# First projection in written order on all five streams, with two raw token tiles, GpSimd scaling the others, and norm weights as columns

## The chip, the core and the metric

The kernel runs on one core of one Trainium2 chip. A core has five instruction streams that run beside each other and wait for each other through semaphores: PE (matmuls, with its weight loads PEld), DVE, ACT, POOL (GpSimd) and SP, which here mostly issues DMAs. The metric is the device time of one execution in microseconds (us); the time of the kernel before is the median of 3 runs.

## The reference

One layer of a decoder block over 1024 tokens of width 1024. Cut to what matters for the change:

```python
h = rmsnorm(x, norm_mix[layer])          # x * rsqrt(mean(x*x) + 1e-6) * g
[q, k/v per NSA branch, gates, rq, rk, rv, rg, gate_a, gate_b] = split(h @ w_in[layer])
q  = rotary(q, positions, 16, 500000.)   # also the NSA keys
rq, rk = rotary(rq, positions, 128, 10000.), rotary(rk, ...) * 128**-0.5
ret = retention(rq, rk, rv)              # chunks of 128 tokens, per-head normalised
ret_out = silu(rg) * ret
mix = sigmoid(gate_a) * (nsa_out @ w_proj_a) + sigmoid(gate_b) * (ret_out @ w_proj_b)
x = x + mix @ w_out
x = x + square(relu(rmsnorm(x, norm_mlp) @ w_up)) @ w_down
y = rmsnorm(x, norm_final)
```

The change concerns the beginning: the first RMSNorm, and `h @ w_in` for the retention heads 0 and 1 (their q and k: "first projection"; their v and g: "second projection").

## The kernel before

**Tiles.** The 1024 tokens are eight tiles of 128 (`NT`), the width 1024 is eight blocks of 128 (`KD`). The normalised input is kept transposed for the whole kernel in two buffers, `bh` and `bl`: `bh` is the value rounded to the matmul's format, `bl` the remainder. Every weight is split the same way into `wh` and `wl` (`chunk_weights`, 512 KB at a time, two width blocks each). A product of float32 accuracy is then three matmuls per width block: bh·wh, bh·wl, bl·wh, so that one token tile against 512 columns is 24 matmuls of 128x512 (`dense_tok`).

**Normalisation of a tile.** `load_norm` loads 128 rows of x. `norm_tile` squares them on ACT with a sum per row (L199), has GpSimd turn the sum into 1/rms (`rstd_of`, `msq` L193 and `rstd` L194), and has DVE multiply x by it and by the gain in one instruction (L203, `h`, 128x1024). The gain is a row, broadcast to all 128 partitions by a DMA of 512 KB (`load_gain`). `to_big` transposes h on PE in eight blocks (L209), four to a PSUM bank `tp`; ACT writes `bh` (L212) and DVE `bl` (L213).

**First projection.** Loop over the eight token tiles. Tiles 0 and 1 advance together, two width blocks at a time, as the weights arrive; `to_big` of tile j+1 stands on PE ahead of the matmuls of tile j. The 128x512 result is scaled by ACT into `xq` (L305, four heads, with the factors `small`), and rotated on DVE into `qk` (`rot_ret`, L314 to L317: two products of 128x512, two sums of 128x256). The rotation's cosines and sines come from tables that GpSimd makes from the positions in `table_steps`: `ang`, `num`, three pairs of `prd` and `ang`, then a clip on DVE, two sines on ACT, and two more GpSimd operations. The retention's tables have 128x512 elements; those of the NSA heads (`cosn`, `sinn`, needed long after) have 128x64.

**Second projection.** Per tile: four width blocks of matmuls, the score matmuls of the tile before (`pS`, `ret_s`), the transposition of `qk` (`ret_t`, split by ACT and DVE into `qkT`, L322/L323), the retention output (`ret_o`), and the other four width blocks. Its weights `w_r0b` are loaded and split by `chunk_weights` after the last tile of the first projection.

**What sets the order.** At the start, 17 warm-up matmuls on zeros run ahead of the data. Inside `manual_schedule` (the first three weight steps of tiles 0 to 2) PE and POOL keep the order in which the code is written; DVE, ACT and SP are ordered by a scheduler there. Behind it the scheduler orders all five. Every engine executes its stream in order, so an instruction that waits holds back all behind it.

Of the kernel before, what the change touches and what calls it, by code (L numbers as in the profile page):

```python
# [111 lines left out]
def hybrid_block(ctx: ExitStack, tc: tile.TileContext, a: dict, out: bass.AP):  # L112
# [84 lines left out]
    def norm_a(x, o, pool):  # L197
        ssq = pool.tile([P, 1], F32, name="ssq", tag="ssq")
        A.activation(o, x, AF.Square, accum_out=ssq)  # L199
        return rstd_of(ssq, D, pool)  # L200

    def norm_b(x, r, gain, o):
        V.scalar_tensor_tensor(o, x, r, gain, op0=OP.mult, op1=OP.mult)  # L203

    def to_big(h, j, ps):
        for q in range(2):
            tp = ps.tile([P, 4, P], F32, name="tp", tag="tp")
            for k in range(4):
                T.transpose(tp[:, k], h[:, (4 * q + k) * P:(4 * q + k + 1) * P], ident)  # L209
            js = slice(j * P, (j + 1) * P)  # L210
            ks = slice(4 * q, 4 * q + 4)
            A.activation(bh[:, ks, js], tp, AF.Copy)  # L212
            V.tensor_sub(bl[:, ks, js], tp, bh[:, ks, js])  # L213

    def load_gain(src, pool, name):
        g = pool.tile([P, D], F32, name=name, bufs=1)
        nc.sync.dma_start(g, src.to_broadcast([P, D]))
        return g

# [23 lines left out]
    with ExitStack() as es:  # L243
        psA = es.enter_context(tc.tile_pool(name="psA", bufs=2, space=PSUM, reuse_waits="tile"))
        tabs = es.enter_context(tc.tile_pool(name="tabs", bufs=1, reuse_waits="tile"))
        cret = tabs.tile([P, 6 * P], F32, name="cret")[:, :P + 512 + 72]
# [8 lines left out]
        with ExitStack() as e1:  # L255
# [21 lines left out]

            def table_steps(part):
                pos = nrm.tile([P, NT], F32, name="pos")
                V.tensor_copy(pos, pos_i)  # L280
                inv0 = P + 512
                for half, off, cos, sin in (((64, 0, cosr, sinr), (8, 64, cosn, sinn))[part],):
                    shp = [P, NT, half]
                    ang = tmp.tile(shp, F32, name=f"ang{half}", tag="t1")
                    num = tmp.tile(shp, F32, name=f"num{half}", tag="t2")
                    prd = tmp.tile(shp, F32, name=f"prd{half}", tag="t1")
                    G.tensor_tensor(ang, pos[:, :, None].to_broadcast(shp),
                                    cret[:, None, inv0 + off:inv0 + off + half].to_broadcast(shp), op=OP.mult)
                    G.tensor_scalar(num, ang, 1.0 / TWO_PI, MAGIC, op0=OP.mult, op1=OP.add)
                    for pc in (PC1, PC2, PC3):  # L290
                        if pc == PC2:
                            yield
                        G.tensor_scalar(prd, num, -MAGIC, -pc, op0=OP.add, op1=OP.mult)
                        G.tensor_tensor(ang, ang, prd, op=OP.add)
                    yield
                    V.tensor_scalar(ang, ang, PI_LO, -PI_LO, op0=OP.min, op1=OP.max)
                    A.activation(sin, ang, AF.Sin)
                    A.activation(num, ang, AF.Sin, scale=0.5)
                    G.tensor_mul(num, num, num)
                    G.tensor_scalar(cos, num, -2.0, 1.0, op0=OP.mult, op1=OP.add)  # L300

            def rot_ret(ps, j, s0, o):
                xq = tmp.tile([P, 512], F32, name="xq")
                for h in range(4):
                    A.activation(xq[:, h * P:(h + 1) * P], ps[:, h * P:(h + 1) * P], AF.Copy,  # L305
                                 scale=small[:, s0 + h:s0 + h + 1])
# [94 lines left out]
            warm = nrm.tile([P, 512], mybir.dt.bfloat16, name="warm", bufs=1)  # L401
            V.memset(warm, 0.0)
            wps = psA.tile([P, 512], F32, name="mm", tag="mm")
            for i in range(WARM):
                mm(wps, warm[:, :P], warm, True, True)
            with tc.manual_schedule(engines={mybir.EngineType.PE, mybir.EngineType.Pool}):
# [1120 lines left out]
```

## Time and profile before

| | |
|---|---|
| median of 3 runs | 1585.05 us (1584.82 to 1585.37) |
| profiled execution | 1585.19 us |
| its span | 1583.4 us |
| granted TensorE clock, mean | 0.995 |
| PE busy | 98% of the span |
| DVE / ACT / POOL busy | 68% / 46% / 27% |

The page's second part shows the same thing by fortieths of the span: PE stands at 7 tenths in the first fortieth and at 9 or more in all others, and PEclk, the granted TensorE clock, at 8 tenths in the first and at 9 or more after it. A fortieth is 39.6 us. Times below count from the start of the span. In the list of groups, a row is: line, engine, operation, output<-inputs, shape, count | busy us, mean ns of one | idle before it and what released it.

### The profile page before, as it was taken

Reading aid. Unit: us, or ns where it says so; the run is one execution under the profiler, and the core shown is the slowest. Engines: PE = TensorE matmul, PEld = TensorE weight load, DVE = VectorE, ACT = ScalarE, POOL = GpSimd, SP = SyncE. Lnnn points to the kernel's source line nnn. Section 1 sums busy time; section 2 is a strip of 40 time slices with the busy share of each in tenths; the row PEclk is TensorE's granted clock in tenths of the full one; section 3 lists DMA queues with packets and bytes.
Section 4 is the critical chain, followed back from the end, with each engine's and each line's share of the span. In section 5 each row is a group of like instructions: output and inputs, shape, how many; then the busy total and the mean of one; then the engine's idle time right before and its main releaser. Section 6 shows DMA issues by size and latency. Waiting matters only on the chain.

```text
span 1583.4 us, 22723 instructions
## 1 busy us (share of the span) xinstructions
PE 1551.3 (98%) x7847; PEld 1297.6 (82%) x7847; DVE 1078.8 (68%) x2208; ACT 730.4 (46%) x1643; POOL 421.2 (27%) x502
## 2 busy tenths in 40 slices
PE   7999999999999999999999999999999999999998
PEld 5888887887888888888888888788888888888886
DVE  5765565683777777776665378777777667876673
ACT  5454454573676776666622144222222244443452
POOL 4111010000332333233100000655554436521320
PEclk8999999999999999999999999999999999999999
DMA  6102101252111111211453332444444497664472
GB/s 224 52 29 67 53 18 43 67 180 70 54 38 45 54 47 34 61 48 61 154 179 118 133 130 89 157 154 159 153 154 159 169 375 252 212 221 121 144 268 98
DMA packets 99363, 191.83 MB, mean 121 GB/s; under 512 B 26864, under 2 KB 30320, under 8 KB 99248
## 3 DMA queue, kind: packets, MB, share of 16 engines
q1 hardware_dynamic: 98144, 187.50, 35.8%
q0 software_dynamic: 560, 1.84, 0.3%
q8 instruction: 62, 1.02, 0.3%
q10 hardware_dynamic: 544, 1.05, 0.2%
q14 instruction: 53, 0.43, 0.1%
HBM read 140.02 MB, written 50.33 MB: 120 GB/s over the span
## 4 chain that ended last, share of the span: by engine, by line
PE 86%; DVE 5%; issue 3%; ACT 3%; POOL 2%; DMA 1%; SPq 0%; POOLq 0%; ACTq 0%; DVEq 0%
PE mmu L159 22%; PE mm L159 20%; PE mmd L159 19%; PE gps L159 9%; PE S L159 4%; PE O L159 3%; PE pt L893 2%; PE pt L892 2%; ACT pW L848 1%; PE pO L159 1%; DVE S L839 1%; PE pc L159 1%; DVE pl L895 1%; ACT pS L848 0%; PE pD L159 0%
## 5 line engine op out<-in xcount | busy, mean ns | idle before, releaser
L1046 DVE TENSOR_TENSOR wl<-raw,wh 128x1024 fp32r<-128x1024 f32 x121 | 182.3, 1531 | 66.6 <-ACT wh L1045 65.1
L1045 ACT ACTIVATE wh<-raw 128x1024 fp32r<-128x1024 f32 x121 | 125.2, 1056 | 206.5 <-PE mmd L159 121.8
L159 PE MATMUL mm<-wh,bh 128*128 128x512 f32 (+1 forms) x448 | 175.6, 392 | 1.2 <-ACT n L580 1.0
L159 PE MATMUL mm<-wh,bl 128*128 128x512 f32 (+1 forms) x448 | 170.2, 380 | 4.8 <-DVE bl L213 4.7
L159 PE MATMUL mmd<-wh 128*128 128x512 f32 x448 | 174.3, 389 | 0.0
L159 PE MATMUL mmd<-wl,wh 128*128 128x512 f32 x448 | 174.3, 389 | 0.0
L159 PE MATMUL mmd<-wh,wl 128*128 128x512 f32 x448 | 174.3, 389 | 0.0
L159 PE MATMUL mm<-wl,bh 128*128 128x512 f32 (+1 forms) x448 | 169.7, 379 | 0.0
L895 DVE TENSOR_TENSOR pl<-pt,ph 128x512 fp32r<-128x512 f32 (+1 forms) x160 | 103.7, 648 | 32.1 <-ACT ph L894 30.1
L894 ACT ACTIVATE ph<-pt 128x512 fp32r<-128x512 f32 (+1 forms) x160 | 90.3, 567 | 55.8 <-PE pt L893 53.9
L839 DVE CUSTOM_DVE_ANT_0 S<-S,edge_m 128x512 f32<-128x512 f32 (+3 forms) x192 | 100.6, 529 | 14.2 <-PE S L159 12.5
L857 POOL TENSOR_SCALAR pS<-pS,cf 128x1024 f32<-128x1024 f32 (+7 forms) x64 | 47.9, 748 | 229.5 <-DVE cf L855 78.2
L159 PE MATMUL gps<-bh,wh 128*128 128x512 f32 x256 | 108.2, 423 | 0.3 <-ACT gst L750 0.2
L159 PEld LDWEIGHTS mm<-wh,bl 128*128 128x128 f32 x448 | 84.8, 189 | 22.2 <-DVE bl L213 5.8
L1127 POOL TENSOR_TENSOR sf<-raw 128x512 f32<-128x512 f32 x14 | 22.7, 1623 | 297.2 <-DVE wl L1046 291.9
L159 PE MATMUL gps<-bl,wh 128*128 128x512 f32 x256 | 100.5, 393 | 0.0
L159 PE MATMUL gps<-bh,wl 128*128 128x512 f32 x256 | 100.5, 392 | 0.0
L159 PE MATMUL mmu<-bh,wh 128*128 128x512 f32 x256 | 99.7, 389 | 0.0
L159 PE MATMUL mmu<-bl,wh 128*128 128x512 f32 x256 | 99.6, 389 | 0.0
L159 PE MATMUL mmu<-bh,wl 128*128 128x512 f32 x256 | 99.6, 389 | 0.0
L159 PEld LDWEIGHTS mmd<-wl,wh 128*128 128x128 f32 x448 | 84.1, 188 | 17.6
L159 PEld LDWEIGHTS mmd<-wh,wl 128*128 128x128 f32 x448 | 84.1, 188 | 17.5
(322 smaller groups left out, 4005.8 us busy)
## 6 DMA issues: line engine op xcount, KB each, us to landing
raw<-u_scr SPq DMA_DIRECT2D x56, 512.0 KB, 4.1
raw<-w_down SPq DMA_DIRECT2D x41, 512.0 KB, 4.7
raw<-w_up SPq DMA_DIRECT2D x32, 512.0 KB, 3.6
u_scr<-u SPq DMA_DIRECT2D x60, 256.0 KB, 2.2
u_scr<-s SPq DMA_DIRECT2D x45, 256.0 KB, 2.0
y<-w_down SPq DMA_DIRECT2D x14, 512.0 KB, 8.3
x<-x SPq DMA_DIRECT2D x8, 512.0 KB, 3.6
qt<-q_scr SPq DMA_DIRECT2D x32, 128.0 KB, 2.4
```

The costliest lines, as they stand in the source:

```text
L159: T.matmul(o, w, m, start=start, stop=stop)
L839: V.tensor_tensor_reduce(sc, sc, mk, -0.125, BIGPOS, OP.add, OP.min, mx[:, b:b + 1])
L848: A.activation(o, sc, AF.Exp, bias=mx[:, m:m + 1], scale=-1.0, accum_out=sums[:, b:b + 1])
L857: G.tensor_scalar(v, v, cf[:, b:b + 1], 1.0, op0=OP.mult, op1=OP.mult)
L892: T.transpose(tp[:, bi * 2], p0, ident)
L893: T.transpose(tp[:, bi * 2 + 1], p1, ident)
L894: A.activation(ph[:, :n], tp[:, :n], AF.Copy)
L895: V.tensor_sub(pl[:, :n], tp[:, :n], ph[:, :n])
L1045: A.activation(h[:, :n], r, AF.Copy)
L1046: V.tensor_sub(l[:, :n], r, h[:, :n])
L1127: eng.tensor_tensor(F[:, 1], x11, x21, op=OP.subtract)
```

## The change

- PE, GpSimd, DVE, ACT and SP all keep the written order to the end of the first projection; the scheduler takes over with the second.
- x is transposed before the gain is applied. The gain comes as 8 rows of 128, is transposed once on PE into eight columns (`gcols`), and DVE multiplies the transposed block by it (`put_half`, `y`, 128x512 twice per tile). ACT then rounds `y` into `bh`, DVE writes `bl` (`split_half`). The 512 KB broadcast is gone.
- Tiles 2 to 7 are multiplied by 1/rms in place by GpSimd (`scale_tile`, 128x1024) ahead of the transposition. DVE's `h` is gone.
- Tiles 0 and 1 are transposed unscaled. Their 1/rms enters where results leave PSUM: in `scaled_x` as a product of `small` with 1/rms (GpSimd), in `ret_v`, and in `rh`. In the second projection, `renorm` puts the factor into `bh` and `bl` of tiles 0 and 1 once their matmuls there are done: GpSimd adds the two parts, DVE multiplies by a transposed row of 1/rms, ACT and DVE split again.
- Warm-up matmuls are 8 and 5 instead of 17. Four x buffers instead of two. Three small loads go out from ACT's queue. Tiles 2, 3, 6 and 7 accumulate in PSUM banks of the retention stage.
- The loads and splits of `w_r0b` are placed by hand: the first at tile 4, the other three at the end, two of them ahead of the rotation of tile 6 and one ahead of that of tile 7.

```diff
-            def norm_tile(j, x):
-                h = nrm.tile([P, D], F32, name="h", bufs=HB)
-                norm_b(x, norm_a(x, h, nrm), gain1, h)
-                return lambda: to_big(h, j, psA)
...
+            def rstd(x):
+                ssq = nrm.tile([P, 16], F32, name="ssq", tag="ssq")[:, :1]
+                A.activation(warm, x, AF.Square, accum_out=ssq)
+                return rstd_of(ssq, D, nrm)
...
+            def put_half(x, j, q):
+                tp = psA.tile([P, 4, P], F32, name="tp", tag="tp")
+                for k in range(4):
+                    T.transpose(tp[:, k], x[:, (4 * q + k) * P:(4 * q + k + 1) * P], ident)
+                y = nrm.tile([P, 4, P], F32, name="y")
+                V.tensor_tensor(y, tp, gcols[:, 4 * q:4 * q + 4, None].to_broadcast([P, 4, P]), op=OP.mult)
+                return y
+
+            def split_half(y, j, q):
+                at = (slice(None), slice(4 * q, 4 * q + 4), slice(j * P, (j + 1) * P))
+                A.activation(bh[at], y, AF.Copy)
+                return lambda: V.tensor_sub(bl[at], y, bh[at])
+
+            def scale_tile(x):
+                G.tensor_scalar(x, x, rstd(x), 1.0, op0=OP.mult, op1=OP.mult)
+
+            def put_tile(j, x):
+                ys = [put_half(x, j, q) for q in range(2)]
+                for lo in [split_half(y, j, q) for q, y in enumerate(ys)]:
+                    lo()
+
+            def renorm(j):
+                js = slice(j * P, (j + 1) * P)
+                tp = psA.tile([P, 4, P], F32, name="tp", tag="tp")
+                T.transpose(tp[:, 0], rs_raw[j].to_broadcast([P, P]), ident)
+                rb = tp[:, :1].to_broadcast([P, 4, P])
+                for q in range(2):
+                    ks = slice(4 * q, 4 * q + 4)
+                    y = tmp.tile([P, 4, P], F32, name="yr", tag="xq")
+                    G.tensor_tensor(y, bh[:, ks, js].bitcast(F32), bl[:, ks, js].bitcast(F32), op=OP.add)
+                    V.tensor_tensor(y, y, rb, op=OP.mult)
+                    A.activation(bh[:, ks, js], y, AF.Copy)
+                    V.tensor_sub(bl[:, ks, js], y, bh[:, ks, js])
...
+            def scaled_x(ps, j, s0):
                 xq = tmp.tile([P, 512], F32, name="xq")
+                sc = small[:, s0:s0 + 4]
+                if s0 == 8 and j < RAW:
+                    sc = sm_raw[j]
+                    G.tensor_scalar(sc, small[:, s0:s0 + 4], rs_raw[j], 1.0, op0=OP.mult, op1=OP.mult)
                 for h in range(4):
...
+                for j in range(2, NT):
+                    if j < NT - 1:
+                        put_tile(j + 1, xs[j + 1])
+                    if j > 2:
+                        banks.append(bank(j))
+                    if j == 3:
+                        ws.append(w_dma(0, "w_r0b"))
+                        W2 = []
...
+                    if j == 4:
+                        w_hi(ws[0])
+                        W2 += w_lo(ws[0])
+                    dense_tok(banks[j], j, W)
+                    if j + 2 < NT:
+                        scale_tile(xs[j + 2])
+                    if j + 4 < NT:
+                        xs.append(load_norm(j + 4))
+                    if j == 3:
+                        for _ in table_steps(1):
+                            pass
...
+                    rotate(scaled_x(banks[j - 2], j - 2, 8), j - 2)
+                for i in (1, 2):
+                    w_hi(ws[i])
+                    W2 += w_lo(ws[i])
+                rotate(scaled_x(banks[6], 6, 8), 6)
+                w_hi(ws[3])
+                W2 += w_lo(ws[3])
+                rotate(scaled_x(banks[7], 7, 8), 7)
...
-                    v, y = ret_v(j, ps)
+                    v, y = ret_v(j, c, ps)
+                    if c == 0 and 0 < j <= RAW:
+                        renorm(j - 1)
```

What this does to the streams is shown at three places. A row is line, operation, output<-inputs, elements; the numbers in names tell buffers apart.

**GpSimd between the scaling of x for tile 4 and that for tile 6, after the change.** x_335 and x_337 are the inputs of tiles 4 and 5, ssq_540 belongs to tile 6; ang8, num8, prd8 are the NSA tables; the two rows that write fac_108 from small_94 are the factors for `xq` of tile 0 and of tile 1.

```order
L274 TENSOR_SCALAR x_335<-x_335,rstd_391 128x1024
L321 TENSOR_SCALAR fac_108<-small_94,fac_108 128x4
L192 TENSOR_SCALAR msq_459<-ssq_457 128x1
L193 TENSOR_TENSOR rstd_460<-msq_459,nhalf_97 128x1
L274 TENSOR_SCALAR x_337<-x_337,rstd_460 128x1024
L301 TENSOR_TENSOR ang8_466<-pos_135,cret_107 128x64
...
L313 TENSOR_SCALAR cosn_111<-num8_467 128x64
L321 TENSOR_SCALAR fac_108<-small_94,fac_108 128x4
L192 TENSOR_SCALAR msq_542<-ssq_540 128x1
```

The same place before, where ssq_489 and ssq_550 are the row sums of two neighbouring tiles:

```order
L193 TENSOR_SCALAR msq_491<-ssq_489 128x1
L194 TENSOR_TENSOR rstd_492<-msq_491,nhalf_97 128x1
L287 TENSOR_TENSOR ang8_374<-pos_372,cret_107 128x64
...
L300 TENSOR_SCALAR cosn_110<-num8_375 128x64
L193 TENSOR_SCALAR msq_552<-ssq_550 128x1
L194 TENSOR_TENSOR rstd_553<-msq_552,nhalf_97 128x1
```

The ten operations of the NSA tables stood between two tiles' 1/rms before; now the scaling and the factor for tile 1's `xq` stand around them, the factor behind all ten.

**ACT at the same place, after.** warm_128 is the scratch that the squares go to, mm_216 and pO_217 are the results of tiles 1 and 2, y_500 and y_507 the halves of tile 5, raw_429 the first part of `w_r0b`, x_395 the input of tile 6.

```order
L252 ACTIVATE warm_128,ssq_457<-x_337 128x1024
L310 ACTIVATE sinn_112<-ang8_466 128x64
L311 ACTIVATE num8_467<-ang8_466 128x64
L323 ACTIVATE xq_482<-mm_216,fac_108 128x128 x4
L343 ACTIVATE n_973<-qk_488 128x2x128
L270 ACTIVATE bh_92<-y_500 128x4x128
L270 ACTIVATE bh_92<-y_507 128x4x128
L455 ACTIVATE wh_431<-raw_429 128x1024
L252 ACTIVATE warm_128,ssq_540<-x_395 128x1024
```

Before, around the NSA sines (mm_390 and mm_451 are results of two neighbouring tiles, tp_435 and tp_442 the transposed halves of a tile):

```order
L305 ACTIVATE xq_416<-mm_390,small_94 128x128 x3
L297 ACTIVATE sinn_111<-ang8_374 128x64
L298 ACTIVATE num8_375<-ang8_374 128x64
L305 ACTIVATE xq_416<-mm_390,small_94 128x128
L212 ACTIVATE bh_92<-tp_435 128x4x128
L212 ACTIVATE bh_92<-tp_442 128x4x128
L199 ACTIVATE h_549,ssq_550<-x_510 128x1024
L305 ACTIVATE xq_477<-mm_451,small_94 128x128 x4
```

The square of the next tile stood behind `bh` before, too; now `xq` ahead of it takes a factor from GpSimd, `bh` comes from DVE's `y`, and a weight split and the rounding of a rotated `qk` (`n`) stand between.

**DVE where the second projection begins, after.** qkT_700 is the transposed `qk` of tile 0; the rows on t1_731 to qk_730, t1_747 to qk_746 and t1_761 to qk_760 rotate tiles 5, 6 and 7; wl_612, wl_671 and wl_724 are the second, third and fourth part of `w_r0b`.

```order
L344 TENSOR_TENSOR qkT_700<-tp_695,qkT_700 128x4x128
L335 TENSOR_TENSOR t1_731<-xq_725,cosr_109 128x512
...
L338 TENSOR_TENSOR qk_730<-t1_731,t2_732 128x4x64
L458 TENSOR_TENSOR wl_612<-raw_609,wh_611 128x1024
L458 TENSOR_TENSOR wl_671<-raw_668,wh_670 128x1024
L335 TENSOR_TENSOR t1_747<-xq_741,cosr_109 128x512
...
L338 TENSOR_TENSOR qk_746<-t1_747,t2_748 128x4x64
L458 TENSOR_TENSOR wl_724<-raw_721,wh_723 128x1024
L335 TENSOR_TENSOR t1_761<-xq_755,cosr_109 128x512
L336 TENSOR_TENSOR t2_762<-xq_755,sinr_110 128x512
```

Before, where t1_663 to qk_657 rotate tile 6, qkT_685 is that of tile 0, wl_714 to wl_726 are the first three parts of `w_r0b`, and t1_736 to qk_730 rotate tile 7:

```order
L314 TENSOR_TENSOR t1_663<-xq_658,cosr_108 128x512
...
L317 TENSOR_TENSOR qk_657<-t1_663,t2_664 128x4x64
L323 TENSOR_TENSOR qkT_685<-tp_680,qkT_685 128x4x128
L238 TENSOR_TENSOR wl_714<-raw_712,wh_713 128x1024
L238 TENSOR_TENSOR wl_720<-raw_718,wh_719 128x1024
L238 TENSOR_TENSOR wl_726<-raw_724,wh_725 128x1024
L314 TENSOR_TENSOR t1_736<-xq_731,cosr_108 128x512
```

Behind the first `qkT` stood three weight splits and one rotation; now three rotations and three splits stand there, alternating.

More of the change, by code (lines that the diff above doesn't have):

```diff
@@ L195, in rstd_of @@
         return r[:, :w]
[L197 to L218, printed above, removed]
     def dense_tok(o, j, W, k0=0, k1=KD, ticks=True):
@@ L278, in table_steps @@
-            def table_steps(part):
[L279 to L294, printed above, removed]
-                    yield
[L296 to L300, printed above, removed]
@@ new lines, in table_steps @@
+            def table_steps(part):
+                half, off, cos, sin = ((64, 0, cosr, sinr), (8, 64, cosn, sinn))[part]
+                inv0 = P + 512 + off
+                shp = [P, NT, half]
+                ang = tmp.tile(shp, F32, name=f"ang{half}", tag="t1")
+                num = tmp.tile(shp, F32, name=f"num{half}", tag="t2")
+                prd = tmp.tile(shp, F32, name=f"prd{half}", tag="t1")
+                G.tensor_tensor(ang, pos[:, :, None].to_broadcast(shp),
+                                cret[:, None, inv0:inv0 + half].to_broadcast(shp), op=OP.mult)
+                G.tensor_scalar(num, ang, 1.0 / TWO_PI, MAGIC, op0=OP.mult, op1=OP.add)
+                for pc in (PC1, PC2, PC3):
+                    yield
+                    G.tensor_scalar(prd, num, -MAGIC, -pc, op0=OP.add, op1=OP.mult)
+                    G.tensor_tensor(ang, ang, prd, op=OP.add)
+                yield
+                V.tensor_scalar(ang, ang, PI_LO, -PI_LO, op0=OP.min, op1=OP.max)
+                A.activation(sin, ang, AF.Sin)
+                A.activation(num, ang, AF.Sin, scale=0.5)
+                G.tensor_mul(num, num, num)
+                G.tensor_scalar(cos, num, -2.0, 1.0, op0=OP.mult, op1=OP.add)
+                yield
@@ L399, in ret_z @@
                 nc.sync.dma_start(b_scr[j, :, 2 * c:2 * c + 2], bt)
[L401 to L406, printed above, removed]
[L407 to L413 removed]
+            eng = mybir.EngineType
@@ L414, in hybrid_block @@
                 steps = table_steps(0)
                 next(steps)
-                W = chunk_weights("w_r0a", 512, 0, 1)
-                xt = load_norm(1)
-                put = norm_tile(1, xt)
-                next(steps, None)
-                first = [psA.tile([P, 512], F32, name="mm", tag="mm") for _ in range(2)]
-                dense_tok(first[0], 0, W, 0, 2)
-                put()
-                dense_tok(first[1], 1, W, 0, 2)
-                W += chunk_weights("w_r0a", 512, 1, 2)
@@ L425, in hybrid_block @@
-                xt = load_norm(2)
-                nc.sync.dma_start(small, a["c_small"])
-                for i in range(1, 4):
-                    if i > 1:
-                        W += chunk_weights("w_r0a", 512, i, i + 1)
-                    for j in range(2):
-                        dense_tok(first[j], j, W, 2 * i, 2 * i + 2)
-                    if i == 1:
-                        put = norm_tile(2, xt)
-                        xt = load_norm(3)
-                    if i == 2:
-                        put()
-                        next(steps, None)
@@ new lines, in hybrid_block @@
+                lb()
+                w_hi(ws[3])
+                next(steps)
+                W += w_lo(ws[3])
+                scale_tile(xs[3])
+                dense_tok(banks[0], 0, W, 4, 6)
+                y2 = [put_half(xs[2], 2, q) for q in range(2)]
+                dense_tok(banks[1], 1, W, 4, 6)
+                dense_tok(banks[0], 0, W, 6, 8)
+                l2 = [split_half(y, 2, q) for q, y in enumerate(y2)]
+                l2[0]()
+                l2[1]()
+                raw_factors(0, xs[0])
```

165 lines of the change are left out of this document (119 added, 46 removed).

## Prediction

> **What bounds the kernel now.** First the page, for the bound; then PE's list of waits over the first 160 us, since behind that point no stream of PE is altered.
>
> ```profile
> span 1583.4 us, 22723 instructions
> PE 1551.3 (98%) x7847; PEld 1297.6 (82%) x7847; DVE 1078.8 (68%) x2208; ACT 730.4 (46%) x1643; POOL 421.2 (27%) x502
> PE mm L159 <- DVE bl L213: 4.7, 1, 4.7
> PE tp L209 <- DVE h L203: 3.2, 2, 2.4
> ```
>
> PE is the bound: 32 us of the span are without it. Of what the change touches it waits 7.9 us (4.7 + 3.2), and pays for it once more in clock. The table by windows (start:end, length, busy of PE, PEld, DVE, ACT, POOL, granted clock, DMA) and PE's timeline (start, duration) show that:
>
> ```profile
> 8.59 1.09 PE L209 MATMUL tp<-ident,h 128*128 128x128 f32 x8 [0.84 <-DVE h L203]
> ...
> 11.54 0.40 PE L159 MATMUL mm<-wh,bl 128*128 128x512 f32 x1
> 14.33 1.94 PE L209 MATMUL tp<-ident,h 128*128 128x128 f32 x8 [2.40 <-DVE h L203]
> ...
> 22.03 0.80 PE L159 MATMUL mm<-wh,bl 128*128 128x512 f32 x1 [4.70 <-DVE bl L213]
> 13.00:14.00 1.00, 0.00 (x0) 0.00 (x0) 1.00 (x1) 0.66 (x1) 1.00 (x1) 0.77 0.36 147
> 14.00:27.00 13.00, 7.96 (x22) 5.99 (x23) 7.65 (x9) 7.50 (x12) 8.89 (x10) 0.50 0.52 187
> 27.00:28.00 1.00, 1.00 (x6) 0.82 (x5) 0.91 (x2) 0.60 (x1) 0.00 (x0) 0.90 0.50 164
> ```
>
> A wait of 2.40 us (11.9 to 14.33) is followed by half clock from about 13.8 (0.77 is the mean of 13 to 14) to 27.4, 5.4 us after matmuls ran on without a gap (22.03). So a wait in this stretch costs its length and then half of PE's work until the clock is back. What there is to win is these waits, the half clock, and nothing more: from tile 3 on PE hardly stops.
>
> ```profile
> 34.54 1.03 PE L209 MATMUL tp<-ident,h 128*128 128x128 f32 x8
> 40.88 1.04 PE L209 MATMUL tp<-ident,h 128*128 128x128 f32 x8
> 47.24 0.60 PE L209 MATMUL tp<-ident,h 128*128 128x128 f32 x4
> 54.20 1.03 PE L209 MATMUL tp<-ident,h 128*128 128x128 f32 x8
> 68.26 0.60 PE L343 MATMUL tp<-ident,qk 128*128 128x128 f32 x4
> 75.55 0.57 PE L159 MATMUL pS<-qkT 128*128 128x256 f32 x4
> 79.46 0.67 PE L159 MATMUL pS<-qkT 128*128 128x256 f32 x4
> ```
>
> These are the marks: the transpositions of tiles 3, 4, 5 and 6, the first `qk` transposition, and the score matmuls of tiles 0 and 1. A tile takes PE 6.35 us (40.88 less 34.54), and from tile 6's transposition to the first pS it is 21.35 us. I follow the changed kernel to the same marks.
>
> **The change, step by step.** Durations by line (busy, mean ns of one, idle before):
>
> ```profile
> L237 ACT ACTIVATE wh<-raw 128x1024 fp32r<-128x1024 f32 x13 | 13.7, 1053 | 7.9 <-DMA raw<-w_r0b 3.1 <-DMA raw<-w_r0a 2.2 <-DMA raw<-w_r1a 1.9
> L238 DVE TENSOR_TENSOR wl<-raw,wh 128x1024 fp32r<-128x1024 f32 x13 | 16.2, 1255 | 1.4 <-ACT wh L237 1.3
> L203 DVE SCALAR_TENSOR_TENSOR h<-x,rstd,gain 128x1024 f32<-128x1024 f32 x8 | 11.0, 1376 | 5.0 <-POOL rstd L194 4.9
> L213 DVE TENSOR_TENSOR bl<-tp,bh 128x512 fp32r<-128x512 f32 x16 | 10.6, 680 | 3.3 <-ACT bh L212 3.3
> L212 ACT ACTIVATE bh<-tp 128x512 fp32r<-128x512 f32 x16 | 8.9, 608 | 5.7 <-PE tp L209 5.7
> L199 ACT ACTIVATE h<-x 128x1024 f32<-128x1024 f32 x8 | 8.5, 1066 | 3.4 <-DMA x<-x 3.4
> L305 ACT ACTIVATE xq<-mm,small 128x128 f32<-128x128 f32 x48 | 13.8, 368 | 20.5 <-issue 12.3 <-PE mm L159 8.2
> L314 DVE TENSOR_TENSOR t<-xq,cosr 128x512 f32<-128x512 f32 x12 | 8.3, 688 | 16.0 <-ACT xq L305 16.0
> L316 DVE TENSOR_TENSOR qk<-t,t 128x256 f32<-128x256 f32 x11 | 4.6, 417 | 0.2
> L193 POOL TENSOR_SCALAR msq<-ssq 128x1 f32<-128x1 f32 x8 | 2.7, 334 | 21.5 <-ACT h L199 21.3
> L194 POOL TENSOR_TENSOR rstd<-msq,nhalf 128x1 f32<-128x1 f32 x8 | 4.5, 557 | 0.7
> L857 POOL TENSOR_SCALAR pS<-pS,cf 128x1024 f32<-128x1024 f32 x8 | 9.0, 1124 | 54.2 <-DVE cf L855 26.7 <-DVE mx L844 17.9 <-ACT ph L894 9.7
> L1128 POOL TENSOR_TENSOR raw<-raw 128x512 f32<-128x512 f32 x14 | 18.9, 1350 | 1.1
> ```
>
> Two operations are new. GpSimd's scaling of x has its form in the L857 row, 1.12 us (ends: 0.6, half of it, and 2.7, twice the half-width two-input row L1128; I take 1.12, the same form). DVE's `y`, 128x512 with one full input, lies between 0.43 (a half-width row, L316, which has two inputs) and 0.69 (L314); I take 0.65, so that 16 of them (10.4) take the place of eight `h` (11.0).
>
> *Start, to tile 3: 8 us won.* `h` goes, so tiles 0 and 1 no longer wait for it, and the 512 KB of the gain no longer stand ahead of x and the weights. GpSimd's table work starts later, for the position cast now stands on DVE behind the two `y` of tile 0. Tile 0's transposition was at 8.59 behind the square (1.1), msq and rstd (0.9) and `h` (1.4): without these at 5.2; with itself (1.1), two `y` (1.3) and the gain's columns (0.5 to 1, an estimate) the cast is there near 8.5. Before, GpSimd's timeline held the tables' first six operations, and one tile's msq and rstd, from the first of these rows to the second:
>
> ```profile
> 6.41 1.05 POOL L287 TENSOR_TENSOR ang<-pos,cret 128x512 f32<-128x512 f32 x1
> ...
> 16.96 0.62 POOL L293 TENSOR_SCALAR prd<-num 128x512 f32<-128x512 f32 x1
> 17.66 1.26 POOL L294 TENSOR_TENSOR ang<-ang,prd 128x512 f32<-128x512 f32 x1
> ```
>
> From 6.41 to 16.96 less the norm's 0.9: 9.6. Started at 8.5, they end near 18; msq, rstd and scaling of tile 2 (0.33 + 0.56 + 1.12 = 2.0) end at 20; the last prd and ang (1.9, up to 3.6 beside DVE) and tile 3's 2.0 end at 24 to 25.6. Tile 3's transposition then starts at about 25.9, against 34.54. Meanwhile PE has the 48 matmuls of tiles 0 and 1, that fit at full clock. Behind it GpSimd does the last two table operations, two tiles' factors and tile 4's scaling: tile 4 at about 33.5, against 40.88, **7.4 us ahead**.
>
> *Tile 4 to tile 5: 8.7 us, where PE needs 6.35.* The stream rows show the circle. `xq` of tile 0 waits for `fac`, which stands on GpSimd behind the scaling of tile 4; `y` of tile 4 stands on DVE behind the rotation of tile 0; `bh` follows `y`; the square of tile 5 follows `bh` on ACT; its scaling follows. From scaling to scaling: fac 0.3, xq 1.2 (four overlap), rotation 2.1 (688 + 688 + 417 + 416 less overlap), two y 1.3, second bh 0.6, square with its sum 1.25, msq and rstd 0.9, scaling 1.1: 8.7 (the square 1.07 and 0.2 as my allowance for reading its sum). Tile 5 starts at 42.2, against 47.24; PE waits 2.3.
>
> *Tile 5 to tile 6: 13.8 us.* The same circle with more in it. The ten NSA operations stand on GpSimd between tile 5's scaling and tile 1's `fac`. Before, they took:
>
> ```profile
> L293 POOL TENSOR_SCALAR prd<-num 128x64 f32<-128x64 f32 x3 | 1.8, 604 | 0.3
> 39.62 0.78 POOL L287 TENSOR_TENSOR ang<-pos,cret 128x64 f32<-128x64 f32 x1
> 40.81 1.33 POOL L293 TENSOR_SCALAR prd<-num 128x64 f32<-128x64 f32 x1
> 45.15 0.61 POOL L300 TENSOR_SCALAR cosn<-num 128x64 f32<-128x64 f32 x1
> ```
>
> 6.1 us from 39.62 to 45.76. Of these 1.1 are one `prd` of 1.33, whose two like ones take 0.24 (1.8 less 1.33, halved): so 5.0, and 4.1 if the waits for DVE and ACT between them shrink too (4.1 to 6.1). And ACT has `wh` of `w_r0b` (1.05) ahead of the square. So 8.7 + 4.1 to 6.1 + 1.05 = 13.8 to 15.8; I take 13.8. What covered these ten before is PE's supply of transposed tiles: GpSimd had nothing to do with h but msq and rstd. Tile 6 starts at 56.0 by that, **1.8 behind** 54.20, and PE waits 7.5 in one piece. Less than 20.7 (13.3 as before, and the 7.4) from tile 4 to 6 would keep it ahead; I get 22.5.
>
> *Clock: 2.5 us.* 7.5 us without a matmul must lower the clock if 2.40 did. The clock came back 5.4 us after the 4.70 wait, so PE works about 5 us at half speed: 2.5 lost (2 to 4). Tile 7's scaling, 7.4 after tile 6's, hides in it. First pS at 56.0 + 21.35 + 2.5 = 79.9, **4.3 behind** 75.55.
>
> *Start of the second projection: 4 us and its clock.* Before, DVE's timeline held one rotation ahead of the first `qkT` and then three splits:
>
> ```profile
> 70.33 0.68 DVE L323 TENSOR_TENSOR qkT<-tp,qkT 128x512 fp32r<-128x512 f32 x1
> 70.93 3.48 DVE L238 TENSOR_TENSOR wl<-raw,wh 128x1024 fp32r<-128x1024 f32 x3
> ```
>
> After, between `qkT` of tile 0 and that of tile 1 stand three rotations (6.3), three splits (3.7), two sums with the mask (0.8) and `qkT` itself (0.7): 11.5, plus up to two GpSimd additions of `renorm` (1.35 each by L1128), which keep DVE's two-input work out while they run (as with the `prd` above): up to 14.2. The first `qkT` ends 2.7 after PE's `qk` transposition (68.26 to 71.01), and PE wants the second 11.2 after it (79.46). So 2.7 + 11.5 to 14.2 less 11.2: PE waits 3.0 to 5.7; I take 4.0 (the later `wh` splits are loaded in time, the last `wl` holds width block 6 for part of it). Half clock can follow: 0 to 2.5, I take 1.5, for the waits here come in two pieces about as long as the 2.40. Together 5.5 (0 if DVE keeps up, 8 at most).
>
> [...]
>
> *Rest.* `renorm` adds two transpositions, eight DVE, four ACT and four GpSimd operations under tiles 1 to 3 of the second projection. DVE's part (4 x 0.69 + 4 x 0.68 = 5.5) lies beside PE, which does not wait there in any row of before; I take 1.0 for the pushed-back `sm` and `qkT` (0 to 3). The later tiles and stages have the same rows on PE and SP: 0.
>
> Sum from the marks: at pS +4.3, second projection +5.5, `renorm` +1.0: 10.8. Since four of these steps were taken at a round value between ends, I put **+10.5**: 1585.19 + 10.5 = 1595.7. The profiled run is 0.14 above the median of 1585.05, which is left in.
>
> **Rivals.** *The head start lasts (faster).* Mechanism: GpSimd and ACT run so far ahead of PE that the circle from tile 4 to 6 hides under PE's matmuls. For it: 7.4 us are won by tile 4, and DVE has nothing of `h` on this path. Against it: the rows of the circle stand in sequence, each waiting for the one ahead. It decides at 20.7 us from tile 4 to 6, and below 18.5 it shows: in 16 us, and with DVE keeping up behind, pS comes 7.4 + 13.3 - 16 = 4.7 early, renorm +1.0: 1581.5. Chance 0.07.
>
> *Even (the pile-up is hidden).* For it: the first four width blocks of tile 0 need only splits that stand early, and a PE that comes late gives DVE time. Against it: the three rotations stand behind `qkT` of tile 0, and that comes with PE. Then only tile 6's delay of 1.8 and renorm count, with the clock kept: 1588; with the circle 1.5 shorter 1586.5. Chance 0.10.
>
> *More clock (slower still).* Waits of 2.3 at tile 5 and in the second projection each lower the clock, and it stays down for a second stretch as from 13.8 to 27.4; PE then loses 3 to 4 more: 1599. For it: 2.40 sufficed once. Against: what tile 5's wait costs is taken up by tile 6's. Chance 0.13.
>
> *Dearer scaling.* GpSimd and DVE hold each other up, and a scaling takes 1.8 instead of 1.12: four of the six stand on the path, 2.7 us, 1598.4; counted with the one above.
>
> **Numbers.** Forecast 0.70, 1595.7, its own range 1591 to 1599. Faster 0.07, even 0.10, more clock 0.13. About 0.2%, 3.2 us, is what a measurement of this kernel can tell from no change. Below 1581.9 falls nearly all of the first rival; of the second, between 1581.9 and 1588.2, most, and some of the forecast's lower end; the rest is slower: 0.07, 0.10, 0.83. For 8 in 10 the range takes in the even case's upper half and both slower ones: 1586.5 to 1600.
>
> **What will show it.** Right: transpositions of tiles 3 and 4 earlier by 7 us or more; PE waiting for GpSimd's scaling at tile 5 (about 2 us) and tile 6 (about 7 us), ACT's `xq` for GpSimd's `fac`; PEclk near 0.5 from about 52 to 61; in the second projection PE waiting for `wl` and `qkT` of DVE for 3 to 6 us. Wrong: tile 6's transposition before 52, no clock drop there, or a first pS before 75; then the circle is shorter than its rows, and the first rival holds. If pS comes at 79 to 80 but the time is within 3 us of before, the second projection absorbed it, and my DVE count is at fault. If the time is past 1600, GpSimd's scaling or its additions cost far more than 1.12 and 1.35.

## The result and the profile after

The changed kernel takes 1595.94 us (median of 4 runs, 1595.16 to 1596.90), the kernel before 1585.21 us beside it: ratio 1.0067, interval 1.0049 to 1.0084. It is 0.67% slower, 10.7 us. The profiled execution has a span of 1594.3 us, 10.9 more than before.

PE's list of waits over the first 170 us of the changed kernel (waiting line <- releaser: us in total, times, longest):

```profile
PE tp L263 <- POOL x L274: 11.3, 4, 7.6
PE pS L158 <- DVE qkT L344: 2.7, 1, 2.7
PE tp L263 <- DMA x<-x: 2.0, 1, 2.0
PE mm L158 <- DVE wl L458: 1.5, 2, 1.1
```

The waits for `h` are gone, and of those for `bl` 0.2 us is left. PE now waits for GpSimd's scaling instead, and in the second projection for DVE. PE's timeline at the marks of the prediction:

```profile
26.95 1.10 PE L263 MATMUL tp<-ident,x 128*128 128x128 f32 x8
34.08 1.09 PE L263 MATMUL tp<-ident,x 128*128 128x128 f32 x8 [0.55 <-POOL x L274]
42.73 1.09 PE L263 MATMUL tp<-ident,x 128*128 128x128 f32 x8 [2.08 <-POOL x L274]
56.94 1.97 PE L263 MATMUL tp<-ident,x 128*128 128x128 f32 x8 [7.65 <-POOL x L274]
80.51 0.57 PE L158 MATMUL pS<-qkT 128*128 128x256 f32 x4
88.38 0.77 PE L158 MATMUL pS<-qkT 128*128 128x256 f32 x4 [2.73 <-DVE qkT L344]
100.77 0.38 PE L425 MATMUL pZ<-ident,z 128*128 128x128 f32 x2
```

and the one of these marks that the prediction did not show of before:

```profile
90.13 0.38 PE L396 MATMUL pZ<-ident,z 128*128 128x128 f32 x2
```

Read against the rows of before, the account is: 7.6 us ahead at tile 3, 6.8 at tile 4, 4.5 at tile 5, then 2.7 behind at tile 6, 5.0 behind at the first pS, 8.9 behind at the second, 10.6 behind at the first pZ. That is the whole loss; behind it little is added (the seventh pZ is at 148.71 against 137.54, 11.2 behind). So the start gave nearly what was forecast, and more than twice of it was lost between tile 4 and the second tile of the second projection.

The clock by windows (the columns as in the prediction; the granted clock stands third from the end):

```profile
50.00:52.00 2.00, 0.00 (x0) 0.00 (x0) 2.00 (x6) 1.40 (x3) 0.00 (x0) 0.82 0.00 0
52.00:54.00 2.00, 0.00 (x0) 0.00 (x0) 1.89 (x3) 2.00 (x3) 0.00 (x0) 0.50 0.02 8
...
88.00:92.00 4.00, 3.62 (x11) 2.99 (x12) 3.48 (x8) 2.62 (x5) 0.00 (x0) 0.60 0.19 47
```

While PE has no matmul at all from 50 to 54, DVE and ACT are busy. Most of what they do there are links of the circle (a chain of operations over several engines that leads from one scaling to the next), one behind the other; `n` and `bl` run beside them. GpSimd's timeline shows what tile 6's scaling waited for:

```profile
41.55 1.12 POOL L274 TENSOR_SCALAR x<-x,rstd 128x1024 f32<-128x1024 f32 x1
42.63 0.30 POOL L301 TENSOR_TENSOR ang<-pos,cret 128x64 f32<-128x64 f32 x1
...
46.59 0.24 POOL L313 TENSOR_SCALAR cosn<-num 128x64 f32<-128x64 f32 x1
46.81 0.28 POOL L321 TENSOR_SCALAR fac<-small,fac 128x4 f32<-128x4 f32 x1
54.31 0.19 POOL L192 TENSOR_SCALAR msq<-ssq 128x1 f32<-128x1 f32 x1 [7.22 <-ACT warm L252]
54.59 0.56 POOL L193 TENSOR_TENSOR rstd<-msq,nhalf 128x1 f32<-128x1 f32 x1
55.25 1.64 POOL L274 TENSOR_SCALAR x<-x,rstd 128x1024 f32<-128x1024 f32 x1
```

From scaling to scaling 13.7 us: the NSA tables (42.63 to 46.83), then `fac`, and then GpSimd idles 7.2 us until ACT's square arrives. What came between stands on ACT's timeline:

```profile
47.12 1.14 ACT L323 ACTIVATE xq<-mm,fac 128x128 f32<-128x128 f32 x4 [0.98 <-POOL fac L321]
50.42 0.42 ACT L343 ACTIVATE n<-qk 128x256 fp32r<-128x256 f32 x1 [2.15 <-DVE qk L338]
51.02 1.23 ACT L270 ACTIVATE bh<-y 128x512 fp32r<-128x512 f32 x2 [0.19 <-DVE y L265]
52.15 1.04 ACT L455 ACTIVATE wh<-raw 128x1024 fp32r<-128x1024 f32 x1
53.10 1.04 ACT L252 ACTIVATE warm<-x 128x1024 bf16<-128x1024 f32 x1
```

`xq` waits for GpSimd's `fac`, `bh` for DVE's rotation and `y`, and the square (L252) stands behind `bh` and the weight split. GpSimd is the engine that PE is shown to wait for, and it is idle itself for half of the time: the releaser in the list is the last link, not the slow one.

The second projection on DVE's timeline, between `qkT` of tile 0 (74.55) and of tile 1:

```profile
81.52 1.52 DVE L338 TENSOR_TENSOR qk<-t,t 128x256 f32<-128x256 f32 x1
82.96 1.21 DVE L458 TENSOR_TENSOR wl<-raw,wh 128x1024 fp32r<-128x1024 f32 x1
...
85.64 1.42 DVE L337 TENSOR_TENSOR qk<-t,t 128x256 f32<-128x256 f32 x1
86.98 0.41 DVE L338 TENSOR_TENSOR qk<-t,t 128x256 f32<-128x256 f32 x1
87.31 0.41 DVE L372 TENSOR_TENSOR sm<-sm,cret 128x256 f32<-128x256 f32 x1
87.65 0.68 DVE L344 TENSOR_TENSOR qkT<-tp,qkT 128x512 fp32r<-128x512 f32 x1
```

DVE idles only 0.34 us there, at 75.2. Two sums of 128x256 last 1.52 and 1.42 where the same sum behind them takes 0.41; GpSimd's two additions of `renorm` stand exactly beside them:

```profile
81.29 1.46 POOL L289 TENSOR_TENSOR yr<-bh,bl 128x512 f32<-128x512 f32 x1 [17.29 <-DVE t L336]
85.52 1.26 POOL L289 TENSOR_TENSOR yr<-bh,bl 128x512 f32<-128x512 f32 x1 [2.76 <-DVE t L336]
```

### The profile page after: what moved, and what is told of

Its sections match the earlier page's. It is cut to its first block, busy times and chain, and to the rows that moved or that the text cites. A ratio compares the mean times of both kernels' runs of the same rounds, so it can differ in the third digit from the quotient of the medians.

```text
span 1594.3 us, 22767 instructions
## 1 busy us (share of the span) xinstructions
PE 1553.0 (97%) x7846; PEld 1298.6 (81%) x7846; DVE 1091.7 (68%) x2224; ACT 732.3 (46%) x1647; POOL 435.5 (27%) x518
## 4 chain that ended last, share of the span: by engine, by line
PE 84%; DVE 6%; ACT 4%; POOL 3%; issue 2%; DMA 1%; ACTq 0%; POOLq 0%; DVEq 0%; SPq 0%
PE mmu L158 22%; PE mm L158 20%; PE mmd L158 19%; PE gps L158 9%; PE S L158 4%; PE O L158 3%; PE pt L1004 2%; PE pt L1003 2%; ACT pW L959 1%; PE pO L158 1%; DVE S L950 1%; DVE pl L1006 1%; PE pc L158 1%; ACT pS L959 1%; PE pD L158 0%
## 5 line engine op out<-in xcount | busy, mean ns | idle before, releaser
L1157 DVE TENSOR_TENSOR wl<-raw,wh 128x1024 fp32r<-128x1024 f32 x121 | 187.5, 1574 | 64.6 <-ACT wh L1156 62.1
L158 PE MATMUL mm<-wh,bh 128*128 128x512 f32 (+1 forms) x416 | 163.4, 393 | 1.0 <-ACT n L691 1.0
L158 PE MATMUL mm<-wl,bh 128*128 128x512 f32 (+1 forms) x416 | 157.8, 379 | 1.5 <-DVE wl L458 1.5
L158 PE MATMUL mm<-wh,bl 128*128 128x512 f32 (+1 forms) x416 | 157.8, 379 | 0.2 <-DVE bl L271 0.2
L158 PEld LDWEIGHTS mmd<-wh 128*128 128x128 f32 x448 | 84.1, 188 | 17.6
```

What stands on the lines that cost most here:

```text
L158: T.matmul(o, w, m, start=start, stop=stop)
L1157: V.tensor_sub(l[:, :n], r, h[:, :n])
```

## The experiments

The theory: (1) a circle of scaling, `fac`, `xq`, rotation, `y`, `bh`, square and scaling, longer than PE's 6.35 us per tile, makes the waits at tiles 5 and 6; (2) half clock follows the longer wait; (3) DVE's queue, with GpSimd's additions, makes the loss in the second projection. Rivals: GpSimd's scaling is slow by itself or beside DVE's work; the second projection waits only because PE comes late and cold. The kernel before took 1586 to 1589 us as a median beside these runs, so the ratios are compared, not the times. All edits are against the changed kernel, which has 1.0067.

**The NSA tables out of the circle** (with `sinn` and `cosn` as their own scratch, the half-angle sine first).

```diff
-                    if j == 3:
-                        for _ in table_steps(1):
-                            pass
...
                     rotate(scaled_x(banks[j - 2], j - 2, 8), j - 2)
+                    if j == 2:
+                        nsa = table_steps(1)
+                        for _ in range(4):
+                            next(nsa)
+                    if j == 3:
+                        next(nsa)
```

> The ten NSA table operations of GpSimd are moved from between the scaling of tile 5 and tile 1's factor to the idle time behind tile 0's factor (about 34 to 40 us), with their clip and sines behind the rotation of tile 1; they get scratch of their own. Theory of the circle (scaling, factor, xq, rotation, y, bh, square, scaling): tile 5 to tile 6 falls from 14.2 us to about 10, PE's wait at tile 6 from 7.6 to about 3, less half clock, time 1590 to 1592.5 against 1595.9. Rival (GpSimd's scaling itself, or its sharing with DVE, is what is slow): the wait stays above 6 us, time 1595 to 1596.

Measured: ratio 1.0037 (1.0024 to 1.0050). PE's timeline:

```profile
43.03 1.97 PE L263 MATMUL tp<-ident,x 128*128 128x128 f32 x8 [2.17 <-POOL x L274]
53.18 1.92 PE L263 MATMUL tp<-ident,x 128*128 128x128 f32 x8 [1.96 <-POOL x L274]
```

Tile 5 to tile 6 falls from 14.2 to 10.2 us, the wait from 7.65 to 1.96, and the first pS is at 76.21 instead of 80.51. The tables were 4 us of the circle. The waits of about 2 us that are left are both followed by half clock here, from 43.0 to 46.5 and from 53.3 to 56.7 (see the last section), which was not expected of them.

**The clock alone.** 30 matmuls whose results nobody reads fill PE's wait at tile 6.

```diff
+                    if j == 5:
+                        hold = psR.tile([P, 2, 2, P], F32, name="pS").rearrange("p a b c -> p (a b c)")
+                        for _ in range(30):
+                            mm(hold, bh[:, 0, :P], W[0][0], True, True)
```

> 30 extra matmuls of 128x512, results unused, stand on PE ahead of tile 6's transposition, where it waits 7.6 us. They measure the clock alone. Theory: tile 6 still starts at 56 to 57, but PEclk stays at 1.00 there, first score matmul about 2.5 us earlier than 80.5 (78), and 0.8 to 2.5 us of that remain at the end, as DVE's queue in the second projection takes some of it: 1593.4 to 1595.1. Rival (the clock costs nothing beside the wait): first score matmul within 0.5 us of 80.5, time 1595.9.

Measured: ratio 1.0051 (1.0036 to 1.0066), overlapping that of the changed kernel. The clock stays at 1.00 from 50 to 62; tile 6 starts at 57.39 and the first pS at 79.36, 21.97 us apart instead of 23.57. So holding the clock saves 1.6 us there, not 2.5, since with a faster PE the scaling of tile 7 is late (0.32 us in the second row):

```profile
57.39 1.09 PE L263 MATMUL tp<-ident,x 128*128 128x128 f32 x8 [0.84 <-POOL x L274]
64.29 1.09 PE L263 MATMUL tp<-ident,x 128*128 128x128 f32 x8 [0.32 <-POOL x L274]
```

And the first pZ is at 100.74, as in the changed kernel (100.77). DVE's queue did not take the difference: the second pS is still 1.1 us sooner (87.24 against 88.38), behind a wait of 2.73 in both. It is gone at the third pS (97.42 against 97.44), since half clock in the second projection lasts from 86.4 to 93.2 in this execution, and from 88.8 to 92.2 in the changed kernel. Whether any of the 1.6 reaches the end is not settled by these runs.

**The square out of the circle.**

```diff
                 for j in range(2, NT):
+                    if j + 2 < NT:
+                        scale_tile(xs[j + 2])
                     if j < NT - 1:
                         put_tile(j + 1, xs[j + 1])
...
                     dense_tok(banks[j], j, W)
-                    if j + 2 < NT:
-                        scale_tile(xs[j + 2])
```

> The square and scaling of tile j+2 are written ahead of tile j+1's transposition in each step, so that the square no longer stands behind bh on ACT; nothing else moves. Theory of the circle: the wait at tile 5 (2.1) goes, the wait at tile 6 falls to 2 to 3 us (the NSA operations still ahead of tile 1's factor), first score matmul near 73.5, 7 earlier; DVE's queue in the second projection still costs about 5, so 1588 to 1590.5. Rival A (that queue is only there because PE comes late and cold): it vanishes too, 1584 or less. Rival B (GpSimd's scaling is slow): waits at tiles 5 and 6 stay, 1594 to 1596.

Measured: ratio 1.0009 (1.0000 to 1.0019). Tile 5 at 41.16 without a wait, tile 6 at 49.72 with one of 2.07, first pS at 71.12, 9.4 us sooner than in the changed kernel (7 were expected; the 2.07 did not lower the clock here). The profiled execution, 1586.87 us, is one of the two fastest of ten, so the trace shows this kernel at its best. By the ratios two moved lines give back 9.2 of 10.7 us, by the medians (1589.23 against 1595.94) 6.7: the circle is broken at its longest link. Rival B falls. Rival A falls too: the second projection still waits, 1.1 for `wl` and 2.7 for `qkT`, with PE early and the clock at 1.00 until 78.8, near the end of the second of these waits. The wait for `qkT` is 2.7 to 2.8 in all of the first four experiments and the changed kernel, whose first pS lies anywhere from 71.1 to 80.5.

**DVE scales instead of GpSimd.**

```diff
-                G.tensor_scalar(x, x, rstd(x), 1.0, op0=OP.mult, op1=OP.mult)
+                V.tensor_scalar(x, x, rstd(x), 1.0, op0=OP.mult, op1=OP.mult)
```

> DVE instead of GpSimd multiplies x by 1/rms (same place in the written order). Theory of the circle: the one link gets no more than 0.6 us shorter, and at the start the scaling stands in DVE's queue; waits at tiles 5 and 6 stay (2 and 6 to 8 us), time 1595 to 1599. Rival B (GpSimd's scaling and its sharing with DVE): waits shrink by half or more, time 1588 to 1592.

Measured: ratio 1.0068 (1.0053 to 1.0083), no gain. The groups of the changed kernel and of this one (us busy, mean ns of one):

```profile
L274 POOL TENSOR_SCALAR x<-x,rstd 128x1024 f32<-128x1024 f32 x6 | 8.9, 1478 | 0.6
```
```profile
L274 DVE TENSOR_SCALAR x<-x,rstd 128x1024 f32<-128x1024 f32 x6 | 4.6, 762 | 6.0 <-POOL rstd L193 6.0
```

The operation itself is on the mean twice as fast on DVE, yet PE waits 9.4 us for it instead of 11.3, 6.24 of them at tile 6 and 2.28 at tile 4, where it was 0.55. A link that gets 0.7 shorter does not shorten a circle of 9 to 14 us by much, and on DVE the scaling waits for GpSimd's 1/rms instead (6.0 us in the row). The first pZ is 0.7 us sooner than in the changed kernel (100.05); why nothing of that reaches the end is not shown.

**DVE's queue in the second projection.** Rotations sooner:

```diff
-                    rotate(scaled_x(banks[j - 2], j - 2, 8), j - 2)
-                for i in (1, 2):
+                    for i in {2: (0,), 3: (1,), 4: (2,), 5: (3, 4), 6: (5,), 7: (6,)}.get(j, ()):
+                        rotate(scaled_x(banks[i], i, 8), i)
+                for i in (1, 2, 3):
                     w_hi(ws[i])
                     W2 += w_lo(ws[i])
-                rotate(scaled_x(banks[6], 6, 8), 6)
-                w_hi(ws[3])
-                W2 += w_lo(ws[3])
                 rotate(scaled_x(banks[7], 7, 8), 7)
```

> Rotations of tiles 4, 5 and 6 are written one step sooner, all three remaining splits of w_r0b ahead of the rotation of tile 7; so between the qkT of tile 0 and of tile 1 DVE has one rotation instead of three. Nothing of the first projection's scaling moves. Theory of the queue: waits at tiles 5 and 6 stay (2.1 and 7.6), first score matmul 80.5 to 81.5, but the wait for qkT of tile 1 (2.7) and the half clock behind it go; from first score matmul to first pZ 16 to 17.5 us instead of 20.3; time 1591 to 1593 where the changed kernel has 1595.9. Rival (the second projection waits since PE comes late, whatever stands in DVE's queue): 20 us there, time 1595 to 1596.

Measured: ratio 1.0047 (1.0034 to 1.0059). From first pS (81.93) to first pZ (97.94) 16.0 us instead of 20.3, and no half clock; the wait for `qkT` is 1.4 instead of 2.7. PE is as late as before (tile 6 at 57.77), so lateness is not the cause of those waits.

**GpSimd's additions to DVE.**

```diff
-                    G.tensor_tensor(y, bh[:, ks, js].bitcast(F32), bl[:, ks, js].bitcast(F32), op=OP.add)
+                    V.tensor_tensor(y, bh[:, ks, js].bitcast(F32), bl[:, ks, js].bitcast(F32), op=OP.add)
```

> renorm's four additions move from GpSimd to DVE, nothing else. If GpSimd's additions hold up DVE's two-input work where the second projection starts (two rows of 1.4 and 1.5 us among 0.4 us rows), those rows fall to 0.42, qkT of tile 1 comes 1 to 2 us sooner, time 1594 to 1595. Rival (renorm costs by its own work): 1595.9 or more, as DVE has 2.7 us more to do.

Measured: ratio 1.0039 (1.0027 to 1.0052), more than expected. The two long sums are now:

```profile
81.03 0.42 DVE L338 TENSOR_TENSOR qk<-t,t 128x256 f32<-128x256 f32 x1
...
84.04 0.42 DVE L337 TENSOR_TENSOR qk<-t,t 128x256 f32<-128x256 f32 x1
```

From the first pS to the second 5.8 us instead of 7.9, and from there to the first pZ 10.8 instead of 12.4, as the clock stays at 1.00: 16.6 instead of 20.3 in all. Of the 5.7 us that the second projection loses against before, 3.7 hang on two additions of GpSimd that were not on any path of their own. DVE's 2.7 us of additional work did not show: the two additions in this stretch stand behind `qkT` of tile 1 there, at 86.37 and 88.08.

**Both cuts of the circle** (the edits of the first and the third experiment).

```diff
+                    if j + 2 < NT:
+                        scale_tile(xs[j + 2])
                     if j < NT - 1:
                         put_tile(j + 1, xs[j + 1])
...
+                    if j == 2:
+                        nsa = table_steps(1)
...
+                    if j == 3:
+                        next(nsa)
```

> Both cuts at once: scaling written ahead of the tile before's transposition, and the NSA operations in GpSimd's idle time. Theory of the circle: no wait over 2 us for GpSimd at tiles 5 and 6, no half clock before the second projection, tile 7's transposition at 54 to 56, first score matmul 69 to 71; the second projection's wait for qkT and wl (4 us with clock) stays, so time 1585.5 to 1588 by the times of the kernel before at 1585.2. If the wait there vanishes as PE is no longer late: 1581 to 1583.

Measured: ratio 1.0021 (1.0012 to 1.0030), first pS at 72.86: no better than the third alone, a miss. One wait of 2.53 is left at tile 6, and in this execution half clock followed it (0.50 at 52 and 53). All four edits together (these, the rotations sooner and the additions on DVE):

> All of it: scaling ahead, NSA operations in idle time, rotations sooner, additions on DVE. Theory: no wait over 2 us from tile 3 to the third pZ, clock 1.00 throughout from 14 us, first score matmul 70 to 71.5, first pZ 85 to 87 against 90.1 before; the head start of 5 us is then kept to the end: 1580 to 1582 where the kernel before has 1585.2 (ratio 0.997 to 0.998). Rival (renorm and the raw tiles cost in the second projection what the start gains): 1584 to 1586.

Measured: ratio 0.9981 (0.9972 to 0.9990), faster than before, but less than the steps promised: first pS at 73.34, first pZ at 87.89. The wait at tile 6 is there still, 2.58, and half clock follows it from 50.8 to 54.2. ACT's timeline of that kernel shows why:

```profile
42.30 1.15 ACT L327 ACTIVATE xq<-mm,fac 128x128 f32<-128x128 f32 x4 [1.02 <-PE tp L263]
45.60 0.42 ACT L347 ACTIVATE n<-qk 128x256 fp32r<-128x256 f32 x1 [2.16 <-DVE qk L342]
45.93 0.24 ACT L314 ACTIVATE cosn<-sinn 128x64 f32<-128x64 f32 x1
46.20 0.26 ACT L315 ACTIVATE sinn<-sinn 128x64 f32<-128x64 f32 x1
46.37 1.04 ACT L252 ACTIVATE warm<-x 128x1024 bf16<-128x1024 f32 x1
```

The two sines (their tables serve as their own scratch, so they read and write `sinn` and `cosn`) need DVE's clip, which stands behind the rotation of tile 1, and the square of tile 6 (L252) stands behind the sines. `n` stands ahead of it as well and waits 2.16 us for the same rotation. With the clip and sines two steps later:

```diff
-                    if j == 3:
+                    if j == 5:
                         next(nsa)
```

> As the run with all four edits, and the clip and sines of the NSA tables, which stand on ACT ahead of the square of tile 6 there and wait for DVE, are written two steps later. Theory of the circle: PE's wait of 2.58 at tile 6 falls below 1, no half clock between 17 us and the third pZ, tile 7's transposition at 56 to 57 instead of 58.3, first pZ 1 to 2.5 us sooner than 87.9; ratio to the kernel before 0.9965 to 0.998. Rival (GpSimd's scaling of tile 6 is late for another reason): the wait stays above 2, ratio as before, 0.998.

Measured: ratio 0.9959 (0.9944 to 0.9974). On ACT the square now stands ahead of `n`, too:

```profile
42.92 1.07 ACT L252 ACTIVATE warm<-x 128x1024 bf16<-128x1024 f32 x1
45.21 0.42 ACT L347 ACTIVATE n<-qk 128x256 fp32r<-128x256 f32 x1 [1.12 <-DVE qk L342]
```

So both of what held the square are out of its way, and the edit does not tell apart what each was worth. Tile 6 starts without a wait, tile 7 2 to 3 us sooner than expected, and the clock is 1.00 from 27 to 124 us:

```profile
47.49 1.16 PE L263 MATMUL tp<-ident,x 128*128 128x128 f32 x8
54.17 1.09 PE L263 MATMUL tp<-ident,x 128*128 128x128 f32 x8
84.99 0.38 PE L429 MATMUL pZ<-ident,z 128*128 128x128 f32 x2
```

This beats both kernels, with all of the change kept but four placements, one engine and the scratch of the NSA tables. The first pZ is 5.1 us ahead of before. All five runs (1581.41 to 1582.84 us) lie below every run of the kernel before (1584.82 and more). How much it is worth is less certain: the ratio says 6.5 us (1585.2 x 0.0041), but the kernel before stood at 1589.24 beside these runs; against its 1585.21 of the result the median is 3.1 us less, and the spans of the two profiled executions differ by 3.6.

## Why the prediction was right

It gave 1595.7; 1595.94 came, and the steps hold one by one, with errors of up to 1 us at single marks and of both signs. That the sum is within 0.3 us of the measurement is closer than the steps are: at the seventh pZ the kernel is 11.2 behind, 0.4 more than the steps add up to, and part of that cancels behind it. It is luck in part, too, since two steps were taken at a value within wide ends (13.8 of 13.8 to 15.8, and 5.5 of 0 to 8).

- *Start*: 7.6 us ahead at tile 3 and 6.8 at tile 4, where 8.6 and 7.4 were forecast (its sign asked for 7 or more at both; tile 4 misses it narrowly). A wait of 2.0 for x of tile 1 and half clock from 10.3 to 13.7 were not in it. What GpSimd's tables waited for was not the cast of the positions, done at 7.9, but the load of the constants `cret`: they began at 9.18 and not at 8.5.
- *Tile 4 to 5*: 8.65 us, forecast 8.7; wait 2.08, forecast 2.3. *Tile 5 to 6*: 14.2, forecast 13.8; wait 7.65, forecast 7.5. From scaling to scaling it is 13.7, and the rest is the longer scaling of tile 6. The first and third experiments show that it is the circle and not one slow operation, and the fourth excludes the scaling's speed.
- *`y` and scaling*: `y` took 0.69 (0.65 taken), the scaling 1.12 to 1.13 where DVE left it alone, 2.21 for tile 2 and 1.64 and 1.66 for tiles 6 and 7. So the price of the last rival (dearer scaling) did occur for three of six tiles; PE waited for the scaling at two of these, tile 2 (1.03) and tile 6.
- *Clock*: half clock from 51.3 to 61.5, forecast from about 52 to 61. From tile 6 to the first pS it took 2.2 us more than before, forecast 2.5; held at full speed it takes 1.6 less.
- *Second projection*: 5.7 us from first pS to first pZ, forecast 5.5, with waits of 2.7 and 1.1 (the other 0.4 for `wl` falls at 15 us) and half clock from 88.8 to 92.2, which is about 1.7 lost; 0.2 is not accounted for. The sum was right; its split was not quite. I put rotations first and counted GpSimd's additions as an extra of up to 2.7 in a range; the fifth and sixth experiments show that either one of the two, removed alone, takes 3.7 to 4.3 of it. The two only cost so much together: with either one removed the wait for `qkT` is 1.4 or 1.7 and the clock stays at 1.00.
- *renorm elsewhere*: 1.0 forecast; 0.5 is what the distance grows between first and seventh pZ.
- The wait at tile 5, forecast as 2.3 and measured as 2.08, did not lower the clock; one of 2.04 at the start of the same run was followed by half clock, from 10.3 to 13.7. That the clock held at tile 5 was luck: in the fifth experiment, where all is the same to that point, a wait of 2.10 there was followed by half clock from 45.0 to 48.4. As the prediction argued, tile 6's wait took that up (6.08 instead of 7.65; 14.2 us from tile 5 to tile 6 in both).

The rivals: the head start did not last, for the reason given against it. The faster rival was priced at 16 us from tile 4 to tile 6 with DVE keeping up behind; the third experiment has 15.0 and still only comes even, since the second projection takes the rest, as the sum had it.

## What to carry to other kernels

When five streams are written out by hand, draw the circle from a buffer's producer back to itself over all engines, with what is queued ahead at each link, and compare its length with the bound engine's time per step: here 8.7 and 13.8 us against 6.35 told the distance of two marks to 0.4 us. Put what depends on nothing (a square of loaded input, a table) ahead of what waits, and not behind it, in every engine's stream: two moved lines were worth 7 to 9 us. An operation off the path beside which one on the path takes longer (GpSimd's additions, and a DVE sum of 1.42 and 1.52 us instead of 0.42) is best kept away from the place where that engine has no spare time.

## What the runs showed of the hardware

Waits of PE of about 2 us go either way: 2.08 (tile 5 of the changed kernel) and 2.07 (tile 6 of the third experiment) left the clock at 1.00; 2.17 and 1.96 in the first experiment were followed by half clock, and so was 2.04 at the start of the changed kernel. The same wait at the same tile in the fifth and in the sixth experiment:

```profile
43.53 1.09 PE L263 MATMUL tp<-ident,x 128*128 128x128 f32 x8 [2.10 <-POOL x L274]
```
```profile
42.28 1.09 PE L263 MATMUL tp<-ident,x 128*128 128x128 f32 x8 [2.10 <-POOL x L274]
```

In the fifth the clock is 0.50 from 45.0 to 48.4, in the sixth it is 1.00 from 14 to 54. What differs between the two is where the wait lies. In the changed kernel the clock changes at 10.3, 13.7, 51.3, 61.5, 88.8 and 92.2 us: 1, 11, 3, 8 and 1 times 3.41 us apart. All 46 changes before 100 us in the profiles of both kernels and of the first eight experiments lie so, whole multiples of 3.41 us apart within each execution, to about 0.05 us; counted from the start of the span, they lie elsewhere in each execution (first at 10.3 in the changed kernel, at 12.3 in the first experiment, at 54.2 in the sixth). Cut by these multiples into stretches of 3.41 us, the profiles hold eleven waits of PE between 1.9 and 2.3 us. Six lie inside one stretch, to within about 0.1 us, and in all six the clock falls at the end of it; five have 0.3 us or more on the far side of an edge, and it holds in all five. In the fifth experiment the wait, 41.43 to 43.53, lies inside the stretch that ends at 45.0; in the sixth, 40.18 to 42.28, an edge at 40.5 cuts 0.3 us off it.

Shorter waits do not sort so well: waits of 1.8 inside one stretch (start of the fourth and the sixth experiment) left the clock up, and the kernel before lost it with only 1.6 of its 2.40 us inside one, among other gaps. Nor does PE's busy share alone: it was at most 0.53 in the stretch ahead of every fall, and at least 0.44 in every other stretch at full clock from 7 us on. Half clock lasted 3.41 us at the shortest and 13.65 at the longest (kernel before), so by an estimate from these a wait of 2 us cost either 2 us or 2 and half of 3.41, that is 3.7. The difference between the third experiment (2.07, cut by an edge, clock up) and the two cuts together (2.53, of which 2.0 lie inside one stretch, clock down) is of this kind, so the latter's miss need not be one of the edit.

Some operations of GpSimd and DVE took longer beside each other. Beside GpSimd's additions (81.29 to 82.75 and 85.52 to 86.78) a DVE sum took 1.52 and 1.42 us instead of 0.42 and ended 0.29 and 0.28 after them; with the additions on DVE, in the sixth experiment, it took 0.42. Beside GpSimd's scaling of tile 6, which took 1.64 instead of 1.12, a DVE product of 128x512 took 1.52 instead of 0.68. In the kernel before, GpSimd's `prd` of 128x64 took 1.33 instead of 0.24 beside DVE's `h` (40.76 to 42.03). Not every pair did so: the two `y` of tile 2 (22.57 to 23.86) took 0.69 and 0.68, where the mean of all sixteen is 0.69, beside a GpSimd product of 1.29 (22.60 to 23.89), which took 1.26 with DVE idle in the kernel before (17.66).
